# Fourth layer of a hybrid decoder trunk: another instruction order in the S5 layers, and weights asked for at other places

## The chip, the core and the metric

The kernel runs on one core of one Trainium2 chip. The metric is the time of one launch in microseconds (us) on the device; lower is better. The core has a matrix engine (PE; PEld is its weight loading), a vector engine (DVE), a scalar engine (ACT), a general engine (POOL) and a queue engine (SP), from whose queue nearly all DMA transfers of this kernel are issued. Each engine works through its own instructions in the order in which the program holds them, and waits at an instruction whose inputs or buffers are not ready.

## The reference

Four layers act on 512 tokens of width 1024. Layers 0 and 3 are S5 layers (a diagonal complex state space model), layer 1 is HGRN2, layer 2 is attention over a window with sinks. Every layer does `h = h + RMSNorm(branch(RMSNorm(h)))`. The S5 branch, cut to what matters:

```python
proj = h @ w_in                       # 1024 -> 2048
u, z = proj[..., :1024], proj[..., 1024:]
# 64 groups of 16 channels, 64 complex states each; (ar, ai) is the discretised pole
xr, xi = einsum(u, bbr), einsum(u, bbi)
sr, si = associative_scan(complex multiply-add with (ar, ai), (xr, xi), over the tokens)
y = einsum(c_re, sr) - einsum(c_im, si) + d_skip * u
y = gelu(y)
y = y * sigmoid(y @ w_glu + b_glu)
return (y * silu(z)) @ w_out
```

## The kernel before

**Products.** Weights are loaded as float32 (`wraw`). Except in the in-projection of layer 0, which multiplies float32 directly, each weight piece is split in two (`w_conv`, lines 174 to 186): ACT writes a rounded part `whi` (line 182), DVE the rest `wlo` (line 183); the activations are split likewise (`xh`, `xl`), and each product is three matmuls (`whi xh`, `whi xl`, `wlo xh`; `ws_steps`, line 228). A weight chunk is 1024 x 256 in two pieces. The pool holds three `wraw` pieces, four `whi` and four `wlo`: two converted chunks. So a new piece can only be loaded when an older piece has been converted (or, in layer 0, used), and a new chunk can only be converted when the chunk two before it has been used.

**An S5 layer.** The in-projection has 8 chunks: 0 to 3 give `u` in eight blocks of 128 channels (b = 0 to 7), 4 to 7 give the gate `z`. The first four blocks are done in two halves of 256 tokens, because the last 256 tokens are normalised and transposed (`xtp`, then ACT `xh` and DVE `xl`, lines 292 to 298) while PE is already at the first 256. Meanwhile each block of `u` goes through the state space model, in these steps:
- `s5_u`: ACT copies the block out (`ut`), a DMA stores it (`ub`) and another loads it in another layout (`u`).
- `s5_v`: a DMA loads the block's parameters (`prm`), DVE and POOL make coefficients (`q`, `q12b`), DVE makes `vt` in three instructions (lines 727 to 731).
- `s5_taps`: PE `kps` and `ktp`, two `tps` transposes that ACT copies to `v`, DVE `ksb` (line 768), and eight small DMAs that write `ksb` into `toep` (line 773).
- `s5_core`: PE `xps`, DVE `xa` and a scan (`r`, line 835), DVE `spre` (line 845), PE `yps` from `toep`, `u`, `w` and `spre` (lines 858, 860), ACT `ysb`, PE `ytp`, ACT `y`.

After the in-projection comes the gate product with `w_glu` (`s5_glu_first` for its first four output blocks, on `yh`, `yl`), then the out-projection.

**What sets the order.** In the S5 layers the order on PE, DVE, ACT and SP is written by a planner, `Flow`: each step above is a generator that names an engine, an assumed duration and the steps it needs; the planner takes the step that could start first by its own clock and emits its instructions. `Flow.free` holds when each engine is free. The transfers of weights are not steps of their own: `w_load` is emitted wherever `w_next` or `w_conv` is called, and so gets a place in SP's queue by the side. In layer 0 the gate's first weights are asked for by `w_next`, when chunk 6 of the in-projection is taken. In layer 3 `s5_convs` (line 620) plans the conversions of chunks 1 to 7; chunk 0 is converted in the out-projection of layer 2 (line 376). That out-projection is ordered by the general scheduler.

Of the kernel before, what the change touches and what calls it, by code (L numbers as in the profile page):

```python
# [50 lines left out]
class Mark:  # L51


    def __init__(self):
        self.t = None


class Flow:
# [6 lines left out]

    LAG = {"P": 0.4, "V": 0.4, "A": 0.4, "G": 0.4, "D": 4.5}

    def __init__(self):
        self.free = dict.fromkeys(self.LAG, 0.0)
        self.lines = []  # L70

    def add(self, line, rank, t=0.0):
# [36 lines left out]
class Trunk:  # L109
# [86 lines left out]
    def w_next(self, name=None):  # L196
        i = self.wi
        if name is not None:
            assert self.wseq[i][0] == name, (self.wseq[i], name)
        self.wi += 1  # L200
        self.w_conv(i)
        self.w_load(i + 1)
        if self.wseq[i][0].endswith("out") and self.wseq[i][2] == 1:
            return self.wcv.pop(i)
        if not self.plain(i) or self.plain(i + 1):
            self.w_conv(i + 1)
            self.w_load(i + 2)
        return self.wcv.pop(i)

    def w_take(self):  # L210
# [117 lines left out]
    def out_proj(self, L, nxt, h):  # L328
# [8 lines left out]
        def evac(ps, c, tb):  # L337
            junk = self.small.tile([P, 512], mybir.dt.bfloat16, tag="junk", name="junk", bufs=1)
            nc.scalar.activation(out=junk, in_=ps, func=AF.Square, accum_out=ss[tb][:, c:c + 1])  # L339
            f = slice(c * 512, (c + 1) * 512)  # L340
            nc.vector.tensor_tensor(out=yg[:, tb, f], in0=ps, in1=gp[:, f], op=ALU.mult)  # L341
# [18 lines left out]
        with self.wx_pool(L):  # L360
            w = []
            for tbs, cs in (((0, 1), (0, 1)), ((2, 3), (0,))):
                for c in cs:
                    if tbs[0] == 0:
                        w.append(self.w_next())
                    for tb in tbs:
                        ps = self.pj("ops")
                        self.as_(ps, self.g, tb, w[c])
                        evac(ps, c, tb)
                if tbs[0] == 0:  # L370
                    for tb in tbs:
                        finish(tb)
                    if nxt is not None:
                        self.norm_stats(nxt, (0, 1), h)
                    spill(0)
            self.w_conv(self.wi)
            self.w_load(self.wi + 1)
            xt = iter(()) if nxt is None else self.norm_xt(nxt, (0, 1))
            next(xt, None)
            for tb in (2, 3):  # L380
                ps = self.pj("ops")
                for k, _ in enumerate(self.as_steps(ps, self.g, tb, w[1])):
                    if k % 4 == 3:
                        next(xt, None)
                evac(ps, 1, tb)
                finish(tb)
                if nxt is not None:
                    self.norm_stats(nxt, (tb,), h)
# [230 lines left out]

    def s5_convs(self, i0, m):  # L620

        for c in range(1, 8):
            yield "A", 2.1, (m["cd", c - 2],) if c > 1 else ()
            yield "V", 2.6, ()
            self.w_conv(i0 + c)
            self.w_load(i0 + c + 1)
            yield m["cv", c]
# [360 lines left out]
    def layer_s5(self, L):  # L988
        nc, a = self.nc, self.a
        j = L // 3  # L990
# [4 lines left out]
        with self.scratch("left"), self.tc.manual_schedule(engines={E.PE, E.DVE, E.Activation, E.SP}):  # L995
            if L:
                self.s5_open(j)
            m = defaultdict(Mark)
            ps, yh, yl, glu = {}, [], [], []

            flow = Flow()
            i0 = self.wi
            if j == 0:
                flow.add(self.s5_tables(j, m), 0, 5.0)
            else:
                m["ap"].t = 4.5
                flow.add(self.s5_convs(i0, m), 60)
            for b in range(8):
                flow.add(self.s5_core(b, m), 10 * b + 1)
# [632 lines left out]
```

## Time and profile before

| | |
|---|---|
| median of 3 runs | 1119.49 us (1118.13 to 1121.62) |
| the profiled execution's own time | 1116.3 us |
| its span, first to last instruction | 1114.5 us |
| PE busy | 1031.2 us |
| DVE busy | 750.5 us |
| ACT busy | 504.2 us |
| mean granted TensorE clock | 0.973 of full |

The busy share of PE counts an engine that works at half clock as busy, so two things lose time there: stretches in which PE waits, and stretches in which the granted clock is low. Both are read from stretches of the trace, below. The profiled execution took 1.8 us outside its span, and is 3.2 us shorter than the median.

### The profile page before, as it was taken

The page shows a single profiled execution, that of the slowest core. Times are in us where ns is not written, and L with a number is a line of the kernel's source. Part 1 is how long each engine was busy: PE and PEld are TensorE (multiplying, and loading weights), DVE is VectorE, ACT ScalarE, POOL GpSimd, SP SyncE. Part 2 cuts the span into 40 slices and gives each one's busy share as a digit, 9 for nine tenths or more (in the row PEclk, how much of TensorE's full clock was granted, in tenths as well). Part 3 has the DMA queues.
Part 4 walks back from the last instruction along what each step waited for, and adds up shares of the span by engine and source line. Part 5 has one row for each costly group of instructions (what it writes and reads, how often), then busy time and mean ns, then how long its engine had stood idle before and what let it go on. Part 6 is the DMA issues. An engine that isn't in the chain of part 4 may idle for free.

```text
span 1114.5 us, 17031 instructions
## 1 busy us (share of the span) xinstructions
PE 1031.2 (93%) x6480; PEld 822.3 (74%) x6480; DVE 750.5 (67%) x1458; ACT 504.2 (45%) x933; POOL 103.2 (9%) x162
## 2 busy tenths in 40 slices
PE   5999975999999999999999898999997879988997
PEld 4755544778899798998978885666676767766876
DVE  6786759585698777887856565556664468863752
ACT  4344425554452314333244534688743355645540
POOL 2000000030200000000011022100002010100200
PEclk9999988999999999999999999999999889998999
DMA  6574233533432324414153452211125357544331
GB/s 230 137 190 126 74 85 98 171 114 126 143 103 81 114 71 132 144 65 151 61 189 124 122 145 62 74 57 53 61 95 167 117 155 238 173 124 146 104 103 57
DMA packets 70577, 133.31 MB, mean 120 GB/s; under 512 B 28896, under 2 KB 40032, under 8 KB 69472
## 3 DMA queue, kind: packets, MB, share of 16 engines
q1 hardware_dynamic: 65664, 119.04, 34.6%
q10 hardware_dynamic: 4832, 13.19, 3.6%
q8 instruction: 51, 0.84, 0.3%
q14 instruction: 30, 0.25, 0.1%
HBM read 100.51 MB, written 20.15 MB: 108 GB/s over the span
## 4 chain that ended last, share of the span: by engine, by line
PE 63%; DVE 15%; ACT 6%; DMA 6%; issue 5%; SPq 2%; POOL 1%; ACTq 1%; DVEq 0%; POOLq 0%
PE pj L228 26%; PE ops L243 13%; PE zps L243 4%; PE vps L243 3%; PE sps L1120 2%; PE scps L1328 2%; DVE wlo L183 2%; SPq L773 2%; ACT whi L182 2%; PE aops L1364 2%; DMA rsw<-rraw 1%; DMA prm<-in_s_bc 1%; PE ptp L1359 1%; DVE sg L1049 1%; PE yps L858 1%
## 5 line engine op out<-in xcount | busy, mean ns | idle before, releaser
L183 DVE TENSOR_TENSOR wlo<-wraw,whi 128x1024 fp32r<-128x1024 f32 x116 | 143.2, 1251 | 65.0 <-ACT whi L182 56.1
L228 PE MATMUL pj<-xh,whi 128*128 128x512 f32 (+1 forms) x496 | 182.3, 370 | 0.0
L228 PE MATMUL pj<-xl,whi 128*128 128x512 f32 (+1 forms) x496 | 177.9, 360 | 2.5 <-DVE xl L298 2.4
L228 PE MATMUL pj<-xh,wlo 128*128 128x512 f32 (+1 forms) x496 | 177.4, 359 | 0.0
L182 ACT ACTIVATE whi<-wraw 128x1024 fp32r<-128x1024 f32 x116 | 120.7, 1056 | 79.4 <-PE pj L228 38.2
L228 PE MATMUL pj<-xf,wraw 128*128 128x512 f32 (+1 forms) x320 | 116.0, 512 | 0.0
L228 PEld LDWEIGHTS pj<-xh,whi 128*128 128x128 f32 x496 | 96.3, 195 | 16.8 <-issue 5.8
L228 PEld LDWEIGHTS pj<-xl,whi 128*128 128x128 f32 x496 | 96.9, 196 | 14.6 <-DVE xl L298 3.2
L228 PEld LDWEIGHTS pj<-xh,wlo 128*128 128x128 f32 x496 | 96.5, 195 | 13.6 <-issue 1.7
L243 PE MATMUL ops<-whi,gh 128*128 128x512 f32 x256 | 101.6, 398 | 2.7 <-ACT gh L1051 2.2
L243 PE MATMUL ops<-wlo,gh 128*128 128x512 f32 x256 | 100.7, 394 | 1.1 <-DVE wlo L183 1.0
L243 PE MATMUL ops<-whi,gl 128*128 128x512 f32 x256 | 100.5, 395 | 0.0
L228 PEld LDWEIGHTS pj<-xf,wraw 128*128 128x128 f32 x320 | 59.2, 192 | 40.4 <-issue 36.7
L243 PEld LDWEIGHTS ops<-whi,gh 128*128 128x128 f32 x256 | 48.2, 188 | 13.8 <-ACT gh L1051 3.0
L243 PEld LDWEIGHTS ops<-wlo,gh 128*128 128x128 f32 x256 | 48.2, 188 | 13.2 <-DVE wlo L183 2.7
L243 PEld LDWEIGHTS ops<-whi,gl 128*128 128x128 f32 x256 | 48.1, 188 | 11.3 <-DVE gl L1052 0.9
L228 PE MATMUL pj<-yl,whi 128*128 128x512 f32 x128 | 51.0, 399 | 3.5 <-DVE yl L950 3.5
L228 PE MATMUL pj<-yh,whi 128*128 128x512 f32 x128 | 51.3, 401 | 0.5 <-ACT yh L946 0.5
L228 PE MATMUL pj<-yh,wlo 128*128 128x512 f32 x128 | 50.8, 397 | 0.0
L341 DVE TENSOR_TENSOR yg<-ops,gpost 128x512 f32<-128x512 f32 x32 | 21.9, 688 | 36.9 <-ACT junk L339 36.6
L243 PE MATMUL vps<-wlo,xh 128*128 128x256 f32 x160 | 45.3, 283 | 0.0
L243 PE MATMUL vps<-whi,xl 128*128 128x256 f32 x160 | 45.3, 283 | 0.0
(279 smaller groups left out, 2106.4 us busy)
## 6 DMA issues: line engine op xcount, KB each, us to landing
wraw<-in_s_in SPq DMA_DIRECT2D x32, 512.0 KB, 6.3
wraw<-in_hg_in SPq DMA_DIRECT2D x32, 512.0 KB, 3.6
wraw<-in_at_in SPq DMA_DIRECT2D x20, 512.0 KB, 4.2
wraw<-in_s_glu SPq DMA_DIRECT2D x16, 512.0 KB, 3.8
wraw<-in_s_out SPq DMA_DIRECT2D x16, 512.0 KB, 3.5
hd<-h SPq DMA_DIRECT2D x6, 1024.0 KB, 4.0
prm<-in_s_bc SPq DMA_DIRECT2D x16, 256.0 KB, 4.6
ub<-ut SPq DMA_DIRECT2D x16, 256.0 KB, 4.2
```

Of the source, the lines that this page charges most:

```text
L182: nc.scalar.activation(out=hi, in_=raw, func=AF.Copy)
L183: nc.vector.tensor_tensor(out=lo, in0=raw, in1=hi.bitcast(F32), op=ALU.subtract)
L228: self.nc.tensor.matmul(ps, lhsT=l[k // 4][:, k % 4, c], rhs=r[:, k, n0:n1], start=k == 0 and n == 0, stop=k == KB - 1 and n == len(terms) ...
L243: self.nc.tensor.matmul(ps, lhsT=l[:, k, c], rhs=r[k // per][:, k % per, :], start=k == 0 and n == 0, stop=k == KB - 1 and n == 2)
L341: nc.vector.tensor_tensor(out=yg[:, tb, f], in0=ps, in1=gp[:, f], op=ALU.mult)
L773: nc.sync.dma_start(out=toep[128 - n:128, jj, :, :], in_=ksb[0:n].rearrange("p a g h -> p (a g) h"))
L858: nc.tensor.matmul(o, lhsT=u[:, g, :], rhs=d["toep"][:, :, g, :], start=True, stop=False)
L1049: nc.vector.tensor_tensor(out=sg, in0=sg, in1=y[:, k, :], op=ALU.mult)
L1120: nc.tensor.matmul(ps[:, c, :], lhsT=k[:, c * 128:c * 128 + 128], rhs=q4[:, c, :, 1, :], start=True, stop=True)
L1328: nc.tensor.matmul(ps[:, bb, lo:256], lhsT=self.q[r, 4 * p + 2 * b2 + bb, qs], rhs=self.k[r, p, ks], start=True, stop=True)
L1359: nc.tensor.transpose(tp[:, f, bb, :], sm[:, bb, f * 128:f * 128 + 128], self.ident)
L1364: nc.tensor.matmul(ops[64 * i:64 * i + 64].rearrange("p b q -> p (b q)"), lhsT=self.v[:, n - 1 + f, kv * 64:kv * 64 + 64], rhs=pts[i][:, f ...
```

## The change

Four edits.
1. In layer 0, `w_next` no longer asks for a chunk that is not of the in-projection when it takes chunk 6; the gate's first chunk is then asked for when chunk 7 is taken.
2. In the out-projection ahead of layer 3, the second chunk of the in-projection (chunk 1) is converted and the third (chunk 2) asked for; `s5_convs` then starts at chunk 2.
3. In layer 3 the planner starts with ACT busy until 12.0 and DVE until 13.0 of its clock.
4. The tables of layer 3 (`m["ap"]`) count as there from 12.0 on, instead of 4.5.

```diff
-    def __init__(self):
+    def __init__(self, **busy):
         self.free = dict.fromkeys(self.LAG, 0.0)
+        self.free.update(busy)
...
-        if not self.plain(i) or self.plain(i + 1):
+        if not self.plain(i):
             self.w_conv(i + 1)
             self.w_load(i + 2)
+        elif self.plain(i + 1):
+            self.w_conv(i + 1)
+            if self.plain(i + 2):
+                self.w_load(i + 2)
         return self.wcv.pop(i)
...
             self.w_conv(self.wi)
             self.w_load(self.wi + 1)
+            if nxt == 3:
+                self.w_conv(self.wi + 1)
+                self.w_load(self.wi + 2)
...
-        for c in range(1, 8):
+        m["cv", 1].t = 0.0
+        for c in range(2, 8):
             yield "A", 2.1, (m["cd", c - 2],) if c > 1 else ()
...
-            flow = Flow()
+
+            flow = Flow() if j == 0 else Flow(A=12.0, V=13.0)
...
-                m["ap"].t = 4.5
+                m["ap"].t = 12.0
```

In layer 0 only SP's queue changes, at one place. Before, the two pieces of the gate's first chunk (`s_glu`) stand ahead of `u` and of the eight `toep` transfers of block 4:

```order
L692 DMA rotf<-rot 64x1024
L152 DMA wraw<-in_s_glu 128x1024 x2
L806 DMA u<-ub 128x512
L773 DMA toep<-ksb 16x128
L773 DMA toep<-ksb 32x128
L773 DMA toep<-ksb 48x128
L773 DMA toep<-ksb 64x128
L773 DMA toep<-ksb 80x128
L773 DMA toep<-ksb 96x128
L773 DMA toep<-ksb 112x128
L773 DMA toep<-ksb 128x128
L706 DMA prm<-in_s_bc 128x512
```

Now, at the same place of the queue:

```order
L701 DMA rotf<-rot 64x1024
L815 DMA u<-ub 128x512
L782 DMA toep<-ksb 16x128
L782 DMA toep<-ksb 32x128
L782 DMA toep<-ksb 48x128
L782 DMA toep<-ksb 64x128
L782 DMA toep<-ksb 80x128
L782 DMA toep<-ksb 96x128
L782 DMA toep<-ksb 112x128
L782 DMA toep<-ksb 128x128
L715 DMA prm<-in_s_bc 128x512
L153 DMA wraw<-in_s_glu 128x1024 x2
```

The weight request moved behind ten transfers, and everything behind it keeps its place. PE, DVE and ACT have the same order as before in layers 0, 1 and 2.

In layer 3 the order of all engines changes. On DVE at its entry stood, behind the last instruction of layer 2 (`xs`), the coefficients and `vt` of block 0 among the sixteen `xl` of the last 256 tokens:

```order
L277 TENSOR_SCALAR xs<-h,rs_r 128x1024
L713 TENSOR_TENSOR q_7805<-prm,co 128x256
L715 TENSOR_TENSOR q_7805<-q_7805,q12b 128x256
L727 TENSOR_TENSOR vt<-ap,q_7805 128x1024
L298 SCALAR_TENSOR_TENSOR xl<-xtp,gpre,xh 128x128 x8
L730 TENSOR_TENSOR t_7874<-ap,q_7805 128x1024
L731 TENSOR_TENSOR vt<-vt,t_7874 128x1024
L298 SCALAR_TENSOR_TENSOR xl<-xtp,gpre,xh 128x128 x8
L713 TENSOR_TENSOR q_7981<-prm,co 128x256
```

Now:

```order
L282 TENSOR_SCALAR xs<-h,rs_r 128x1024
L303 SCALAR_TENSOR_TENSOR xl<-xtp,gpre,xh 128x128 x16
L722 TENSOR_TENSOR q_7926<-prm,co 128x256
L724 TENSOR_TENSOR q_7926<-q_7926,q12b 128x256
L736 TENSOR_TENSOR vt<-ap,q_7926 128x1024
L739 TENSOR_TENSOR t_7973<-ap,q_7926 128x1024
L740 TENSOR_TENSOR vt<-vt,t_7973 128x1024
L184 TENSOR_TENSOR wlo<-wraw,whi 128x1024 x2
L722 TENSOR_TENSOR q_8068<-prm,co 128x256
```

All sixteen `xl` come first. On ACT the sixteen `xh` come first likewise. On PE, block 0's `kps` and first `tps` moved from the first half block behind the `xl` to the last one. ACT's and DVE's conversions of chunks 0 and 1 stand at the same places as before: the scheduler already had chunk 1's in the out-projection; what is new there is that SP asks for chunk 2.

SP's queue around block 0's `toep` in layer 3, before (the row behind the last one shown is the second of the eight `toep` transfers):

```order
L613 DMA rotf<-sd 64x1024 x4
L152 DMA wraw<-in_s_in 128x1024 x2
L617 DMA w<-sd 128x1024
L706 DMA prm<-in_s_bc 128x512
L802 DMA ub<-ut 128x8x64
L617 DMA w<-sd 128x1024
L773 DMA toep<-ksb 16x128
```

and now:

```order
L621 DMA rotf<-sd 64x1024 x4
L811 DMA ub<-ut 128x8x64
L625 DMA w<-sd 128x1024
L153 DMA wraw<-in_s_in 128x1024 x2
L715 DMA prm<-in_s_bc 128x512
L815 DMA u<-ub 128x512
L811 DMA ub<-ut 128x8x64
L815 DMA u<-ub 128x512
L153 DMA wraw<-in_s_in 128x1024 x2
L625 DMA w<-sd 128x1024
L811 DMA ub<-ut 128x8x64
L782 DMA toep<-ksb 16x128
```

Block 1's `prm` moved behind a weight request (chunk 3), and block 0's `toep` behind a further one (chunk 4) and the transfers of `u` for blocks 0 and 1. Block 2's `prm` stands behind that `toep` in both; before, one weight request lies between them, now none.

## Rows read from the trace of the kernel before

**Rows 1.** The page's busy times by engine, and of its costliest groups the two of the weight conversion: line, engine, operation, shapes, count, busy us, mean ns of one, idle time before it and what ended most of that.
```profile
PE 1031.2 (93%) x6480; PEld 822.3 (74%) x6480; DVE 750.5 (67%) x1458; ACT 504.2 (45%) x933; POOL 103.2 (9%) x162
...
L183 DVE TENSOR_TENSOR wlo<-wraw,whi 128x1024 fp32r<-128x1024 f32 x116 | 143.2, 1251 | 65.0 <-ACT whi L182 56.1
...
L182 ACT ACTIVATE whi<-wraw 128x1024 fp32r<-128x1024 f32 x116 | 120.7, 1056 | 79.4 <-PE pj L228 38.2
```

**Rows 2.** PE in time around block 4's `yps` in layer 0: start us, length us, engine, line, operation, out<-in, shapes, count, and in brackets the idle time just before with what ended it.
```profile
140.85 1.12 PE L228 MATMUL pj<-xf,wraw 128*128 128x512 f32 x2
149.59 0.69 PE L858 MATMUL yps<-toep,u 128*64 128x128 f32 x4 [7.62 <-DMA toep<-ksb]
```

**Rows 3.** SP's queue in time in the same stretch: start us, time that the issue took with its wait, line, transfer, count.
```profile
122.83 19.52 SPq L152 DMA_DIRECT2D wraw<-in_s_glu  x2
142.40 0.42 SPq L806 DMA_DIRECT2D u<-ub  x1
142.91 5.00 SPq L773 DMA_DIRECT2D toep<-ksb  x8
```

**Rows 4.** The chain of waits in the same stretch: start us, length us, what.
```profile
147.32 1.88 DMA toep<-ksb
149.19 12.11 issue
...
175.51 2.01 ACT whi L182 x2
```

**Rows 5.** DVE in time in the same stretch, columns as in rows 2.
```profile
131.84 0.29 DVE L768 TENSOR_TENSOR ksb<-ktp,dmx 128x128 f32<-128x128 f32 x1 [6.01 <-PE ktp L762]
...
141.37 0.68 DVE L845 TENSOR_TENSOR spre<-r,rsw 128x504 f32<-128x504 f32 x1
...
148.51 0.68 DVE L684 TENSOR_TENSOR rot<-rot,rt 128x512 f32<-128x512 f32 x1
...
161.31 0.29 DVE L768 TENSOR_TENSOR ksb<-ktp,dmx 128x128 f32<-128x128 f32 x1 [12.11 <-issue]
```

**Rows 6.** Stretches: from:to, length, then busy us (x instructions) of PE, PEld, DVE, ACT, POOL, then the granted clock as a share of full, DMA share and GB/s.
```profile
149.50:154.00 4.50, 4.41 (x36) 4.11 (x37) 0.00 (x0) 0.60 (x1) 0.00 (x0) 0.51 0.17 51
...
862.00:874.00 12.00, 8.65 (x47) 7.17 (x48) 7.91 (x17) 4.09 (x12) 0.62 (x1) 0.50 0.23 89
...
905.40:911.00 5.60, 5.51 (x29) 3.83 (x31) 4.95 (x7) 0.74 (x2) 0.00 (x0) 0.50 0.57 138
...
1015.40:1021.00 5.60, 5.52 (x13) 4.38 (x14) 4.24 (x8) 2.09 (x5) 0.00 (x0) 0.51 0.44 157
```

**Rows 7.** PE in time at the entry of layer 3, columns as in rows 2; the first row is the last matmul of the first half blocks.
```profile
856.68 0.28 PE L228 MATMUL pj<-xh,wlo 128*128 128x256 f32 x1
861.83 1.11 PE L292 MATMUL xtp<-cst,xs 128*128 128x128 f32 x4 [4.87 <-DVE xl L298]
864.44 1.12 PE L292 MATMUL xtp<-cst,xs 128*128 128x128 f32 x4 [1.50 <-DVE xl L298]
...
867.54 0.58 PE L228 MATMUL pj<-xl,whi 128*128 128x256 f32 x1 [1.76 <-DVE xl L298]
```

**Rows 8.** DVE in time at the same place, columns as in rows 2.
```profile
852.28 0.89 DVE L277 TENSOR_SCALAR xs<-h,rs_r 128x1024 f32<-128x1024 f32 x1 [2.12 <-POOL rs_r L254]
856.53 0.43 DVE L713 TENSOR_TENSOR q<-prm,co 128x256 f32<-128x256 f32 x1 [3.37 <-DMA prm<-in_s_bc]
```

**Rows 9.** Stretches, columns as in rows 6: from the end of the first half blocks to the end of the second half blocks (96 matmuls of 256 columns) in layers 1, 2 and 3.
```profile
303.96:320.85 16.89, 14.31 (x106) 14.03 (x107) 14.73 (x59) 12.60 (x25) 0.00 (x0) 0.90 0.17 55
620.04:637.78 17.74, 14.35 (x107) 14.11 (x107) 8.33 (x21) 9.95 (x22) 0.00 (x0) 0.90 0.21 55
856.96:884.90 27.94, 19.73 (x148) 17.92 (x149) 16.68 (x28) 10.43 (x25) 2.40 (x3) 0.76 0.43 123
```

**Rows 10.** PE in time at the end of the last of these stretches (`kps` and `tps` at full clock), then at the next long wait; columns as in rows 2.
```profile
883.71 0.64 PE L745 MATMUL kps<-vt,c 128*32 128x128 f32 x16
...
884.74 0.60 PE L754 MATMUL tps<-cst,vt 128*128 128x128 f32 x4
...
905.49 1.08 PE L745 MATMUL kps<-vt,c 128*32 128x128 f32 x16 [5.32 <-DVE vt L731]
```

**Rows 11.** SP's queue between these, columns as in rows 3.
```profile
885.35 1.24 SPq L152 DMA_DIRECT2D wraw<-in_s_in  x2
886.69 0.39 SPq L706 DMA_DIRECT2D prm<-in_s_bc  x1
```

**Rows 12.** DVE's wait for that transfer, columns as in rows 2.
```profile
894.61 0.42 DVE L713 TENSOR_TENSOR q<-prm,co 128x256 f32<-128x256 f32 x1 [10.79 <-DMA prm<-in_s_bc]
```

**Rows 13.** DMA issues of layer 3 up to 1010 us: transfer, queue, count, KB each, median us from issue to landing.
```profile
prm<-in_s_bc SPq DMA_DIRECT2D x8, 256.0 KB, 6.3
```

**Rows 14.** What SP's queue waited for from 840 to 1010 us: us in total, times, longest us.
```profile
SPq L773 <- DVE ksb L768: 22.7, 7, 6.0
...
SPq L152 <- DVE wlo L183: 11.3, 3, 6.4
```

**Rows 15.** The rest of layer 3's in-projection: a stretch (columns as in rows 6).
```profile
915.00:1011.00 96.00, 88.62 (x810) 70.20 (x808) 66.87 (x84) 58.27 (x92) 8.61 (x11) 1.00 0.61 185
```

**Rows 16.** PE in time where the gate product begins, columns as in rows 2.
```profile
1011.53 0.49 PE L228 MATMUL pj<-yh,whi 128*128 128x512 f32 x1 [0.49 <-ACT yh L946]
1015.48 0.80 PE L228 MATMUL pj<-yl,whi 128*128 128x512 f32 x1 [3.45 <-DVE yl L950]
```

## The prediction, made before the changed kernel was run

> **What bounds the kernel now.** I read the page first, then the waits in stretches, then the engines in time around each long wait. The page says PE is busy 93% of the span [rows 1], so a change of order can only win where PE waits or works at a low clock. I listed PE's waits over the two S5 layers, since only these change. In layer 0 there are two long ones. The first, 7.62 us, ends when block 4's `toep` lands [rows 2]; the second is DVE's own work, and no edit touches it. In layer 3 there are four places: the entry, where 4.87, 1.50 and 1.76 us end with an `xl` [rows 7]; a 5.32 us wait for `vt` [rows 10]; 7.4 us of small waits from 915 to 1011 (96 less 88.62) [rows 15]; and 0.49 and 3.45 us where the gate product begins [rows 16]. After each long one the granted clock is about half, 1.2 in place of 2.4 GHz, for some microseconds of work [rows 6].
>
> **Layer 0: the request moves behind `toep`.** The reader should see in SP's rows that the request for the gate weights stood in the queue from 122.83 for 19.52 us, until 142.4 [rows 3]. That is just behind the last matmul of chunk 6, which ends at 141.97 [rows 2]: the second piece needs that chunk's buffer. Behind it waited `u` and `toep`, although `ksb`, the source of `toep`, was done at 132.1 [rows 5]. So `toep` was issued from 142.91 for 5.00 us, landed 1.88 us after the last issue [rows 3, 4], and PE stood still from 141.97 to 149.59.
>
> Now `toep` comes first. It can be issued from 132.1 to 137.1 and lands near 139.0, 3 us before PE comes to `yps`. `spre`, which `yps` also needs, ends at 142.05 [rows 5], so `yps` starts at 142.0 to 142.1. That removes 7.5 us. The half clock behind the wait goes too, since PE no longer stops: 4.41 us of work at 0.51 [rows 6] is 2.2 us. Sum: 9.7 us.
>
> Does it carry to the end? Chain and DVE rows agree: DVE stands idle for 12.11 us until the next `ksb`, at 161.31, which hangs on PE [rows 4, 5]; from there DVE is the engine that everything waits for. All of that starts earlier by what PE wins. The next thing late would be DVE itself, whose work before ends at 149.2; with 9.7 us won `ksb` comes at 151.6, so 2.4 us are left and the cap of the gain is 12.1. The request itself now waits behind `prm`, but for the same buffer until the same 141.97, and its data are first used by a conversion at 175.51 [rows 4], 166 with the gain, so I cost it at nothing; without that cover it would cost its landing, a few us. Behind the waiting request stand block 7's `u` and block 6's rotations; both wait for things that are done at 142 or later anyhow. If `toep`'s landing took longer by its slack of 3 us, the gain would shrink from there; I bound it from below at 6 us.
>
> **Layer 3, the entry.** Before, DVE ends `xs` at 853.17 and could make the first `xl`, but it holds `q` first, which waits until 856.53 for `prm`, and then `vt` [rows 8]. PE is through its first half blocks at 856.96 and waits [rows 7]. Layers 1 and 2 begin in the same way with nothing between the `xl`: there the second half blocks end 16.89 and 17.74 us after the first ones; in layer 3 it is 27.94 us [rows 9]. I take 17.3 for the new order, with its own dip of the clock in it (0.90 in both). Layer 3's 27.94 held block 0's `kps`, two `tps`, `ktp` and block 1's `kps`; now `kps` and one `tps` stay in it, 1.0 us, and about 1.2 us of the others come later (0.64 and 0.60 each at full clock [rows 10]; overlaps make it a little less). Gain: 27.9 - 17.3 - 1.0 - 1.2 = 8.4 us, by the two examples 8.0 to 8.8; the half blocks end near 875.3.
>
> **Layer 3, the next wait.** Before, block 2's `prm` is issued at 886.69, behind two pieces of weights [rows 11], DVE waits for it until 894.61 [rows 12], and PE until 905.49. Cost: 5.32 us and 5.51 us of work at half clock [rows 6], 2.8 us; 8.1 together. Now block 2's `prm` stands behind block 0's `toep`, this behind `ksb`, and that behind the conversion of chunk 3, which can begin when chunk 1's last product is done at 875.3. ACT first copies a `v`, which I put at 878.0, two matmul groups and a copy later; two `whi` of 1.06 to 880.1; the last `wlo`, 1.25 [rows 1], to 881.4; the first `vt` instruction, of the same size, to 882.6; `ksb` 0.3 to 882.9; eight issues 5.0 to 887.9; `u`, then `prm` from 888.5. With the median of 6.3 us [rows 13] it lands at 894.8. DVE's `q` stands ahead of `spre` of block 0, some 3.3 us in all (0.42 twice with POOL between, three of 0.68): `spre` at 898.1. PE did 48 wide matmuls and what lay between them from 884.90 to 900.17, 0.32 us each; now 63 come before that `yps`, so PE is there at 895.4 and waits 2.7 us. With the 7.9 us that the same transfer took here [rows 11, 12] it is 4.3, with 4 us nothing. Next, block 1's `toep` stands behind the request for chunk 5, which waits for the conversion of chunk 4: a wait that can reach the 6.4 us of the longest such wait in this layer [rows 14]; I take 3. With one half-clock dip of 2.8 the new waits are 8.5 in place of 8.1: I take no change, from 8 us better (both hidden) to 6 worse (both at their ends, two dips).
>
> On the clock: here it fell to half after the waits of 4.87, 5.32 and 3.45 us [rows 6, 7, 10, 16]. The Trainium skill, TensorE: Matmul & The Clock Gate, section "What's actually happening", says that the throttled state is the default and activity releases it; by that rule a new wait can bring the dip back even where it is shorter than the old one, and both waits would be paid with a dip, 2.8 us more than in my sum.
>
> **Layer 3, the rest.** The same work in another order over some 96 us, and 3.9 us with 5.52 at half clock (2.7) at the end. DVE is 70% busy and PE 92% [rows 15], so neither side is tight. I take no change, 5 us either way. The earlier request for chunk 2 is worth nothing by itself: it adds two issues to a queue that stands until the layer's tables may be written.
>
> **Sum.** -9.7 - 8.4 = -18.1 us on the profiled execution's 1116.3 gives 1098.2. That execution is 3.2 us below the median of the runs, so I forecast 1101 for the median. Its own range, with 6 to 12.1 in layer 0, 8.0 to 8.8 at the entry and the two open terms within 5 us together, is 1094 to 1109.
>
> **Rivals.**
> - *Only layer 0 counts.* The entry's gain is handed back in layer 3, because the waits for `prm` and `toep` hang on SP and DVE and not on PE. For it: 22.7 us of SP's waits there are for `ksb` and 11.3 for conversions [rows 14]. Against it: these waits also start from PE's progress, which is earlier. Time: 1119.5 - 9.7 = 1110.
> - *The new order works throughout.* The two new waits are hidden (8 us) and half of the small ones go (4 us): 1101 - 12 = 1089. For it: no work of the state space model stands ahead of an `xl` any more. Against it: the planner still gives the weights no time in SP's queue, and those are what the two waits hang on.
> - *Slower: weight requests block `toep` in layer 3.* The mechanism of layer 0 returns there, since in SP's new order a request stands within five rows ahead of `toep` in most blocks (the part on the change shows the first). Each such block costs what it cost in layer 0, 9.7 us. Two are 19.4 and eat the gain; from three on, 1101 + 29 = 1130, the kernel is slower. For it: SP asks for `toep` only behind them (the part on the change). Against it: of the old order's waits for conversions the longest was 6.4 us. The Trainium skill, Trace Analysis, section "What "DMA-bound" means", names the issuing engine's sequencer as a bound of its own when its track is solid; eight issues of 5.0 us for `toep` [rows 3] are 40 us in a layer of 170, so the trace does not show it solid.
> - *The change does not free `toep`.* Something else in front of it in SP's queue holds it until 142. Against it: once the request was out, `u` and `toep` were issued without a further wait, and `ksb` had been done for ten us [rows 3, 5]. Layer 0 then gives nothing: 1119.5 - 8.4 = 1111.
>
> **How the numbers follow.** Forecast 0.46, only layer 0 0.22, works throughout 0.20, slower 0.07, does not free 0.05. A measurement here can tell 0.3%, about 3.4 us, from no change. The first three and the last lie below 1116 with nearly all their weight; I leave 0.03 of "only layer 0" for a loss in layer 3 that cancels: faster 0.90, same 0.03, slower 0.07. The range reaches from the second rival to a little beyond the first: 1089 to 1112.
>
> **What would show it.** Layer 0: PE's wait of 7.62 us gone, `toep` issued near 132, the next `ksb` near 152 instead of 161, the clock full there. Layer 3: DVE's sixteen `xl` without `vt` between, about 17 us from half blocks to half blocks; a wait of 2 to 4 us at the first `yps`, released by `spre`, with DVE waiting for `prm` before. Wrong would be a wait for `toep` in layer 0 that stays, or PE waits in layer 3 that add up to more than before's 25 us.

## The result, and the profile after

The changed kernel takes 1093.64 us (median of 4 runs, 1091.99 to 1095.69); the kernel before took 1119.28 beside it (4 runs, 1118.13 to 1121.62). The ratio is 0.9769, with a 95% interval of 0.9746 to 0.9792: 25.6 us faster. The profiled execution took 1091.99 us, its span is 1090.2 us (before: 1114.5), the mean granted clock 0.982 (before: 0.973). The forecast was 1101 with a range of 1089 to 1112.

The page's busy times, to hold against [rows 1]:

```profile
PE 1025.8 (94%) x6480; PEld 817.1 (75%) x6480; DVE 750.4 (69%) x1458; ACT 505.2 (46%) x933; POOL 101.5 (9%) x162
```

PE executes the same 6480 matmuls and is busy 5.4 us less, which fits less work at half clock; the other 18.9 us of the span were PE standing idle. So the question is which waits went.

**Layer 0.** SP's queue in time (start us, time that the issue took with its wait, line, transfer, count), against [rows 3]:

```profile
132.01 5.00 SPq L782 DMA_DIRECT2D toep<-ksb  x8
137.12 0.52 SPq L715 DMA_DIRECT2D prm<-in_s_bc  x1
137.69 4.50 SPq L153 DMA_DIRECT2D wraw<-in_s_glu  x2
```

`toep` is issued at 132.01 instead of 142.91, and the request for the gate weights, now behind it, still ends only at 142.19: it waits for the same buffer as before. PE in time at that place, against [rows 2]:

```profile
140.71 1.13 PE L233 MATMUL pj<-xf,wraw 128*128 128x512 f32 x2
141.76 0.44 PE L867 MATMUL yps<-toep,u 128*64 128x128 f32 x4
```

No bracket stands behind `yps`: the wait of 7.62 us is gone. DVE, against the last of [rows 5]:

```profile
151.45 0.29 DVE L777 TENSOR_TENSOR ksb<-ktp,dmx 128x128 f32<-128x128 f32 x1 [2.40 <-issue]
```

The next `ksb` comes at 151.45 instead of 161.31, and of DVE's idle 12.11 us before it 2.40 are left.

**Layer 3.** Stretches of the changed kernel (columns as in rows 6): the first is the one behind layer 0's old wait, the second runs from the end of the first half blocks to the end of the second [rows 9], the others follow the three long waits that are left in layer 3.

```profile
149.50:154.00 4.50, 4.50 (x42) 2.62 (x42) 2.44 (x5) 2.18 (x4) 1.16 (x2) 1.00 0.62 126
...
844.36:862.20 17.84, 15.87 (x124) 13.76 (x125) 10.40 (x19) 8.77 (x19) 0.19 (x1) 1.00 0.57 161
...
898.00:901.50 3.50, 3.43 (x33) 3.29 (x33) 3.46 (x4) 0.00 (x0) 0.00 (x0) 0.55 0.86 213
...
953.50:957.00 3.50, 3.41 (x22) 2.48 (x22) 3.33 (x6) 0.39 (x1) 0.62 (x1) 0.50 0.36 118
...
988.00:992.00 4.00, 3.40 (x29) 3.07 (x30) 4.00 (x7) 1.30 (x4) 0.00 (x0) 0.50 0.35 125
```

The granted clock is the column behind POOL's: full in the first two stretches, which stood at 0.51 and 0.76 before, and about half in the other three. PE in time (the first row at the entry, against [rows 7]; then the new order's long waits, against [rows 10, 16]):

```profile
846.88 0.66 PE L297 MATMUL xtp<-cst,xs 128*128 128x128 f32 x4 [1.96 <-DVE xl L303]
...
882.36 0.44 PE L869 MATMUL yps<-w,spre 128*64 128x128 f32 x4 [0.28 <-DVE spre L854]
...
898.07 0.69 PE L867 MATMUL yps<-toep,u 128*64 128x128 f32 x4 [2.69 <-DMA toep<-ksb]
...
953.59 1.08 PE L754 MATMUL kps<-vt,c 128*32 128x128 f32 x16 [3.66 <-DVE vt L740]
...
988.60 0.70 PE L869 MATMUL yps<-w,spre 128*64 128x128 f32 x4 [5.28 <-DVE spre L854]
```

The entry's waits of 4.87, 1.50 and 1.76 us have become one of 1.96. Block 0's `yps` waits 0.28 us, block 1's 2.69. The two long waits further on are new; in return the gate product's first matmuls no longer wait 3.45 us for `yl`. All of PE's listed waits behind the last `xs` ahead of layer 3 add up to 16.5 us, where before they were 26.8.

### The profile page after: what moved, and what is told of

Same layout as the page of the kernel before. It is cut to its first block, busy times and chain, and to the rows that moved or that the text cites. A ratio compares the mean times of both kernels' runs of the same rounds, so it can differ in the third digit from the quotient of the medians.

```text
span 1090.2 us, 17036 instructions
## 1 busy us (share of the span) xinstructions
PE 1025.8 (94%) x6480; PEld 817.1 (75%) x6480; DVE 750.4 (69%) x1458; ACT 505.2 (46%) x933; POOL 101.5 (9%) x162
## 4 chain that ended last, share of the span: by engine, by line
PE 66%; DVE 16%; ACT 6%; DMA 5%; issue 4%; POOL 1%; SPq 1%; ACTq 1%; DVEq 0%; POOLq 0%
PE pj L233 27%; PE ops L248 13%; PE zps L248 4%; DVE wlo L184 3%; PE sps L1130 3%; PE scps L1338 2%; PE vps L248 2%; ACT whi L183 2%; PE aops L1374 2%; PE yps L867 2%; PE yps L869 2%; PE ptp L1369 1%; DMA rsw<-rraw 1%; DVE sg L1059 1%; PE tps L763 1%
## 5 line engine op out<-in xcount | busy, mean ns | idle before, releaser
L233 PE MATMUL pj<-xl,whi 128*128 128x512 f32 (+1 forms) x496 | 175.4, 355 | 0.8 <-DVE xl L303 0.6
L233 PE MATMUL pj<-xh,wlo 128*128 128x512 f32 (+1 forms) x496 | 175.2, 354 | 0.0
L233 PEld LDWEIGHTS pj<-xl,whi 128*128 128x128 f32 x496 | 94.7, 191 | 13.2 <-DVE xl L303 2.2
```

Of the source, the lines that this page charges most:

```text
L233: self.nc.tensor.matmul(ps, lhsT=l[k // 4][:, k % 4, c], rhs=r[:, k, n0:n1], start=k == 0 and n == 0, stop=k == KB - 1 and n == len(terms) ...
```

## How the time splits over the kernel

DVE's rows in time give two landmarks that every kernel here has: the first `xs` of layer 1, and the last `xs` ahead of layer 3 (852.28 before [rows 8]). They cut a span into three legs: layer 0, layers 1 and 2, layer 3. In the changed kernel they are these:

```profile
265.27 1.42 DVE L282 TENSOR_SCALAR xs<-h,rs_r 128x1024 f32<-128x1024 f32 x2 [2.28 <-POOL rs_r L259]
...
839.68 0.88 DVE L282 TENSOR_SCALAR xs<-h,rs_r 128x1024 f32<-128x1024 f32 x1 [2.12 <-POOL rs_r L259]
```

The table has all fourteen traces; the experiments are described below.

| kernel | median us | ratio to before | layer 0 | layers 1, 2 | layer 3 |
|---|---|---|---|---|---|
| before | 1119.2 to 1120.4 | 1 | 274.0 | 578.3 | 262.2 |
| changed | 1093.64 | 0.9769 | 265.3 | 574.4 | 250.5 |
| changed, run again | 1095.99 | 0.9798 | 265.4 | 582.5 | 249.5 |
| edit 1 alone | 1110.54 | 0.9911 | 263.9 | 581.5 | 263.0 |
| half of the request moved | 1112.22 | 0.9925 | 264.8 | 579.9 | 262.1 |
| edits 2 to 4 | 1105.86 | 0.9864 | 273.9 | 579.5 | 249.3 |
| edit 2 alone | 1119.97 | 1.0004 | 273.1 | 579.0 | 265.6 |
| edits 3 and 4 | 1124.77 | 1.0047 | 274.6 | 579.3 | 271.5 |
| edits 2 and 4 | 1115.03 | 0.9968 | 273.4 | 580.9 | 261.3 |
| edits 2 and 4, requests planned | 1098.15 | 0.9821 | 273.8 | 583.0 | 243.4 |
| changed, states first | 1094.47 | 0.9790 | 264.9 | 577.1 | 248.9 |
| changed, requests planned | 1090.64 | 0.9751 | 265.0 | 579.0 | 246.2 |
| changed, both trials | 1088.57 | 0.9729 | 265.5 | 576.6 | 243.1 |
| changed without edit 3, requests planned | 1089.54 | 0.9731 | 265.1 | 579.6 | 243.3 |

Leg 1 has two values and nothing between: 273.1 to 274.6 without edit 1 (mean 273.8), 263.9 to 265.5 with it (mean 265.0). That is 8.8 us. Leg 3 is 262.1 to 263.0 where layer 3 is as before (mean 262.5) and 249.3 to 250.5 where it is as changed (mean 249.8): 12.7 us. Leg 2 holds the same 3496 matmuls in every kernel but that with edits 3 and 4, which does 18 of them later, and lies anywhere from 574.4 to 583.0.

## The experiments

**Edit 1 alone.**

```diff
-        if not self.plain(i) or self.plain(i + 1):
+        if not self.plain(i):
             self.w_conv(i + 1)
             self.w_load(i + 2)
+        elif self.plain(i + 1):
+            self.w_conv(i + 1)
+            if self.plain(i + 2):
+                self.w_load(i + 2)
```

> The kernel before with only the later request for the gate weights (layer 0's edit); layer 3 stays as before. Theory: the request stood in SP's queue ahead of toep because its second piece waited for a buffer; behind toep it costs nothing, so PE's wait of 7.62 us goes with the half clock behind it. The trace of the changed kernel puts DVE's work after it 9.85 us earlier; alone the edit then gives 9.0 to 10.5 us, a time of about 1109.5, and layer 3's entry still lasts 27.9 us from the first half blocks to the second. Rival A: the further 2.7 us that appeared in layer 2 belong to this edit: 12 to 13 us, 1107, with the shift growing from 9.85 to 12.5 between 660 and 690 us in this trace too. Rival B: part of layer 0's gain is lost again at layer 3's entry, because DMA landings there do not move with PE: 5 to 8 us.

Measured: 1110.54 us, ratio 0.9911 (0.9886 to 0.9936), 9.7 us below the 1120.27 of the kernel before beside it. Layer 0's leg has its gain, layer 3's (263.0) none, and the stretch from half blocks to half blocks still has waits of 4.92 and 1.51 us for `xl`. Rival A falls: layers 1 and 2 took 581.5 us here, not less than before. Layer 3's leg shows nothing lost, so rival B falls too.

**Half of the request moved.** The first piece of the gate's chunk, whose buffer is free, stays ahead of `toep`; only the second, which needs chunk 6's, moves.

```diff
+    late = False
...
-        for v in range(pieces):
+        for v in range(len(have), pieces):
+            if (name, j, c, v) == ("s5_glu", 0, 0, 1) and not self.late:
+                self.late = True
+                return
```

> The kernel before with the request for the first gate chunk left where it was, but cut in two: the first piece, whose buffer is free, is asked for at the old place, and only the second, whose buffer is chunk 6's, behind block 5's toep. Theory (the wait for the buffer blocks the queue, not the request as such): toep is issued near 134.5 (one more issue of 2.3 us ahead of it than in the changed kernel) and lands near 141.5 before PE comes; gain 9 to 10.5 us, as in the run with the whole request moved. Rival (the issues and the bytes themselves delay toep, wherever the buffer stands): the gain is about half, 4 to 6 us, with a wait for toep of 3 us or more left at 142.

Measured: 1112.22 us, ratio 0.9925 (0.9897 to 0.9952), and layer 0's leg is 264.8 us, like with the whole request moved: 8.1 us by the medians and 9.0 by the mean of the legs, at the lower end of the 9 to 10.5 expected. SP's queue of this kernel:

```profile
122.32 0.56 SPq L157 DMA_DIRECT2D wraw<-in_s_glu  x1
123.41 0.79 SPq L811 DMA_DIRECT2D u<-ub  x1
131.64 5.01 SPq L778 DMA_DIRECT2D toep<-ksb  x8
136.76 0.52 SPq L711 DMA_DIRECT2D prm<-in_s_bc  x1
141.50 0.33 SPq L157 DMA_DIRECT2D wraw<-in_s_glu  x1
```

The first piece costs the queue 0.56 us and delays nothing; the second sits until 141.5, when its buffer comes free. Of the 19.52 us of [rows 3], all but about one was that one buffer. (That one issue takes 2.3 us, as the expectation had it, was wrong: the 4.50 us of the changed kernel are mostly this wait too.)

**Edits 2 to 4, without edit 1.**

```diff
-            flow = Flow()
+            flow = Flow() if j == 0 else Flow(A=12.0, V=13.0)
...
-                m["ap"].t = 4.5
+                m["ap"].t = 12.0
```

with edit 2 as in the change.

> The kernel before with all edits but the request's: chunk 1 converted and chunk 2 asked for in the out-projection, tables at 12.0, ACT and DVE busy at entry. Theory: the gains add, layer 3 gives what the changed kernel's trace has beyond layer 0 and layer 2, 11 to 13 us, a time of about 1107.5; PE still waits 7.6 us for toep in layer 0, the sixteen xl are uninterrupted, the stretch from half blocks to half blocks lasts 17.8 us. If layer 2's 2.7 us belong to these edits: 14 to 15 us. Rival (layer 3's gain needs layer 0's, because parameters and rotations land relative to another clock): under 8 us.

Measured: 1105.86 us, ratio 0.9864 (0.9817 to 0.9912), 14.4 us between the medians. Layer 3's leg is 249.3 us, layer 0's is as before. The two ratios multiply to 0.9911 x 0.9864 = 0.9776; the changed kernel has 0.9769. The terms add, and the two layers don't need each other. The 14.4 us is at the upper end of what was expected, with an interval that reaches from 10 to 20 us; the leg says 12.9.

**Edit 2 alone.**

```diff
+            if nxt == 3:
+                self.w_conv(self.wi + 1)
+                self.w_load(self.wi + 2)
...
-        for c in range(1, 8):
+        m["cv", 1].t = 0.0
+        for c in range(2, 8):
```

> The kernel before with only the edit that converts chunk 1 and asks for chunk 2 in the out-projection of layer 2; the planner's numbers stay as before. Theory: DVE and PE keep the order of before at the entry, q and a vt stand between xs and the xl, PE waits there as before, and nothing is won: ratio to before 0.997 to 1.003, the stretch from half blocks to half blocks near 28 us. Rival (layer 3's gain comes from the earlier request of chunk 2, so that its conversion and the queue behind it come sooner): 5 us or more faster, though q still stands ahead of the xl.

Measured: 1119.97 us, ratio 1.0004 (0.9980 to 1.0028). By itself the earlier request is worth nothing. (In its one trace layer 3's leg is even 3.1 us longer than the mean of the three with layer 3 as before; the medians don't show that loss.)

**Edits 3 and 4 without edit 2.** The planner's numbers only; chunk 1 is then converted behind the busy time.

> The kernel before with only the planner's numbers (ACT busy to 12, DVE to 13, tables from 12.0), without converting chunk 1 in the out-projection. Its conversion is then planned behind the busy time and stands, with block 0's q and whole vt, ahead of the first of the sixteen xl. Theory: what counts at the entry is that nothing stands between xs and the xl; here q still waits for prm until about 856.5, two wlo of 1.25 and three vt instructions of 1.2 follow, the first xl comes near 863 instead of 861.8 with two wlo's time between, and the second halves end 2 to 5 us later than before: a loss at the entry, the whole between 1117 and 1124 (0 to 5 us slower). Rival (the busy times alone make the better order, the conversion's place does not matter): 8 us or more faster than before.

Measured: 1124.77 us, ratio 1.0047 (1.0022 to 1.0071): slower, as expected, but the expectation had the wrong wait. It spoke of a late first `xl`; the long wait is PE's, earlier, for chunk 1 itself. PE and then ACT in time:

```profile
859.43 0.58 PE L229 MATMUL pj<-xh,whi 128*128 128x256 f32 x1 [7.50 <-ACT whi L183]
```

```profile
858.03 0.40 ACT L719 ACTIVATE c<-prm,cst 128x128 f32<-128x128 f32 x1 [4.58 <-DMA prm<-in_s_bc]
858.34 1.99 ACT L183 ACTIVATE whi<-wraw 128x1024 fp32r<-128x1024 f32 x2
```

The conversion stands behind a coefficient that waits for `prm`, and PE runs out of converted weights in the middle of the first half blocks. So edit 2, worth nothing alone, is what allows edit 3.

**Edits 2 and 4, without the busy times.** As the changed layer 3, but with `Flow()`.

> The kernel before with chunk 1's conversion in the out-projection and the tables' time at 12.0, but without ACT and DVE taken as busy at entry. By the order of the program DVE's sixteen xl then stand together too; what differs from the layer 3 edits together is the planner's order from block 2 on. Theory (the gain is the uninterrupted xl at the entry): 9 to 15 us faster than before, like the layer 3 edits together (14.4 us by the medians), with a stretch of about 17.8 us. Rival (it is the busy times that place requests and toep well after the entry): at least 6 us less than those, with a wait of 3 us or more for prm or toep between 880 and 910 that the changed kernel doesn't have.

Measured: 1115.03 us, ratio 0.9968 (0.9947 to 0.9988), 4.2 us faster by the medians: about 10 less than with edit 3 (12.0 less by layer 3's legs, 261.3 and 249.3). My theory falls here, and the rival stands, though the wait that it named, 3 us or more between 880 and 910, was 2.46 us there and the longer ones came later. The entry is as good as in the changed kernel (the sixteen `xl` start at 856.10, 1.8 us behind the last `xs`, with nothing between), and the gain is given back later. The waits of PE from 850 to 1040 us in this kernel (us in total, times, longest):

```profile
PE yps L862 <- DMA toep<-ksb: 15.5, 5, 3.9
PE kps L749 <- ACT z L940: 3.8, 1, 3.8
PE xtp L292 <- DVE xl L298: 2.0, 1, 2.0
```

Five waits for `toep`. SP's queue ahead of one of them, DVE's `ksb` there, and PE:

```profile
920.88 6.21 SPq L152 DMA_DIRECT2D wraw<-in_s_in  x2
927.14 5.01 SPq L777 DMA_DIRECT2D toep<-ksb  x8
```

```profile
922.14 0.27 DVE L772 TENSOR_TENSOR ksb<-ktp,dmx 128x128 f32<-128x128 f32 x1
925.50 2.36 DVE L183 TENSOR_TENSOR wlo<-wraw,whi 128x1024 fp32r<-128x1024 f32 x2 [3.09 <-ACT whi L182]
```

```profile
934.50 0.44 PE L862 MATMUL yps<-toep,u 128*64 128x128 f32 x4 [3.81 <-DMA toep<-ksb]
```

`ksb` is done at 922.4, but SP holds the request until `wlo` frees a raw buffer, and issues `toep` 4.7 us later; PE then waits 3.81. This is layer 0's mechanism, the one that the prediction carried as its slower rival. Three of the five waits (3.81, 3.46 and 3.92 us) have such a request directly ahead of `toep`; ahead of the first stands a `u` that was issued only at 890.46, and the last, of 1.86 us, follows a late `ksb`.

**The same with requests planned.** Each request becomes a step of its own behind its conversion, so the planner knows that it holds the queue.

```diff
             self.w_conv(i0 + c)
+            yield m["cv", c]
+            yield "D", 0.4, ()
             self.w_load(i0 + c + 1)
-            yield m["cv", c]
```

> The kernel that kept only 3.6 us of layer 3's gain (chunk edit and tables' time, ACT and DVE free at entry), with each request for a weight chunk made a step of its own behind its conversion. In that kernel PE waited for toep five times, 2.46, 3.81, 3.46, 3.92 and 1.86 us. Theory (there the requests, which wait in SP's queue for conversions, stood ahead of toep; the busy times at entry gain because they make the planner put toep first): with requests planned, toep stands ahead of them and the waits for toep fall to 3 us or less in all; time 1103 to 1108, like the layer 3 edits together (ratio 0.984 to 0.992). Rival (without the busy times DVE itself is late with ksb, vt and spre, and toep is late with them): the waits stay at 8 us or more, 1111 to 1116.

Measured: 1098.15 us, ratio 0.9821 (0.9794 to 0.9847), faster than either forecast. PE's waits in the same stretch as above:

```profile
PE pj L228 <- DVE yl L955: 3.3, 1, 3.3
PE xps L826 <- ACT v L761: 3.1, 2, 2.8
PE xtp L292 <- DVE xl L298: 2.0, 1, 2.0
```

No wait for `toep` is left of 15.5 us, and layer 3's leg falls from 261.3 to 243.4 us. The rival (DVE late by itself) falls. Other steps moved with the requests, so not all of the 17.9 us is shown to be the five waits and their half clock.

**Two trials at the changed kernel's waits, and both.** "States first" puts the gate product's second conversion behind block 7's states; "requests planned" is the edit above, on the changed kernel.

```diff
-            yield "V", 2.6, (m["rest"],)
+            yield "V", 2.6, (m["rest"],) + ((m["states", 7],) if early else ())
```

> The changed kernel with the gate product's second conversion and its steps put behind block 7's states, so that spre of block 7 isn't made late by two whi and two wlo ahead of it (PE waited 5.28 us there). Theory (what stands ahead of rsw and spre on ACT and DVE is all of that wait): rsw comes about 2 us earlier, wlo of 2.5 us goes behind spre, PE's wait falls to 1 to 3 us; the conversion late by as much may cost the gate product up to 2 us: 0 to 4 us faster than the changed kernel, 1090 to 1094. Rival (the wait only moves to the gate product, as before the change, where yl was late): the same time, with a new wait of 3 us or more at its first matmuls.

> The changed kernel with each request for a chunk of the in-projection made a step of its own for the planner, on the DMA queue, so that SP's order puts toep of block 1 ahead of the request for chunk 5 (PE waited 2.69 us for that toep at 898). Theory (the request blocked it, as in layer 0): that wait goes with its half clock, 3 to 5 us; the planner moves other steps of layer 3 too, 4 us either way: 1085 to 1096. Rival (toep is late because ksb is): the wait stays at 2 us or more.

> The changed kernel with both trials together: requests planned as their own step, and the gate product's second conversion behind block 7's states. Theory (the two waits, 2.69 us for toep and 5.28 us for spre, have causes of their own): no wait for toep at block 1 as with the first alone, the wait for spre near 3.2 us as with the second alone; 2 to 5 us faster than the changed kernel in the same call. Rival (what is won ahead is waited for at the gate product): within 1 us of the first trial alone, 1090.6.

Measured, in ratios to before: 0.9790 (0.9753 to 0.9826), 0.9751 (0.9717 to 0.9785), 0.9729 (0.9702 to 0.9756). The first alone can't be told from the changed kernel. Its wait for `spre` fell from 5.28 to 3.19 us (1 to 3 were expected), and no new wait of 3 us, as its rival had it, stands behind that one:

```profile
989.44 0.69 PE L869 MATMUL yps<-w,spre 128*64 128x128 f32 x4 [3.19 <-DVE spre L854]
```

The second removed the wait of 2.69 us for block 1's `toep`, as expected: SP asked for it at 888.68, right behind its `ksb` (done at 888.65), where in the changed kernel 2.0 us lay between the two (889.21 and 891.25). With both, the kernel took 1088.57 us beside 1095.99 for the changed kernel, 7.4 us faster where 2 to 5 were expected, with 3.04 us of the wait for `spre` left. That is more than the two alone seem to give (by the legs 0.9 and 3.6 us alone, 6.7 together), but the first one's interval holds 4 us either way.

**The changed kernel again.**

> The changed kernel again, unchanged, beside the two runs below on the same chip. Theory and rivals alike: 1091 to 1097 us, ratio to before 0.974 to 0.980. It tells in a second trace which numbers belong to the program (layer 0's shift of 9.85 us, the stretch of 17.8 us, the waits for toep, vt and spre in layer 3) and which to one execution (layer 2's 2.7 us, prm's landing of 3.1 us).

Measured: ratio 0.9798 (0.9771 to 0.9826). Layer 0's and layer 3's legs come back within 1.0 us, layers 1 and 2 take 582.5 us instead of 574.4. The waits of layer 3 come back as well: 1.96, 2.67, 3.66 and 5.00 us. `prm` of block 2 is issued at 884.49 and used at 887.61, 3.1 us, as in the first trace.

**Requests planned, without the busy times.** The run with edits 2 and 4 and planned requests, plus edit 1; the only difference between the two kernels lies in SP's queue in layer 0.

> The changed kernel with requests planned as their own step, and with ACT and DVE no longer taken as busy at entry; it differs from the run with the tables' time and planned requests only by layer 0's edit. Theory (the terms add; with requests planned the busy times have nothing left to do): the 9.9 us of layer 0 come off that run's ratio of 0.9821, so 0.9733, near 1089 us, like the run with both trials. Rival (the busy times are still worth something, or the terms don't add): 1094 us or more.

Measured: 1089.54 us, ratio 0.9731 (0.9705 to 0.9756). The terms add once more, and with the requests planned the busy times of edit 3 have nothing left to do. The fair neighbour is the changed kernel with requests planned, which differs in the busy times alone: its ratio is 0.9751, the same within the intervals, and layer 3's leg is 246.2 us with them and 243.3 without, so in these two traces they rather cost something.

## Why the prediction was right, and where its sizes were off

**Layer 0 (forecast 9.7 us).** Right in every step: `toep` issued at 132.01 (forecast 132.1), `yps` at 141.76 (142.0), no dip (clock 1.00), the next `ksb` at 151.45 (151.6), 2.40 us left on DVE (2.4). At that `ksb` the trace is 9.86 us ahead; at layer 1's first `xs` 8.7, and over all traces 8.8. The half request shows the cause: not the request as such, but the buffer for which it waits at the head of the queue. About a microsecond is lost on the way, where nothing was forecast to hold it. The traces show where. In both kernels PE waits 9.11 us for a `vt`, still 9.85 us apart; then comes half clock, and the clock's mean over the next 8 us is 0.80 before and 0.62 after the change (PE before and after, then the two stretches, columns as in rows 6):

```profile
188.21 1.08 PE L745 MATMUL kps<-vt,c 128*32 128x128 f32 x16 [9.11 <-DVE vt L731]
178.36 1.08 PE L754 MATMUL kps<-vt,c 128*32 128x128 f32 x16 [9.11 <-DVE vt L740]
...
188.21:196.21 8.00, 7.92 (x96) 6.45 (x97) 7.66 (x10) 4.35 (x7) 0.00 (x0) 0.80 0.01 3
178.36:186.36 8.00, 7.93 (x91) 6.51 (x91) 6.44 (x8) 3.08 (x6) 0.00 (x0) 0.62 0.01 2
```

So the half clock lasted about 3.2 us before and 6.0 now, and the shift falls from 9.85 to 8.66 us by the next `yps` that waits. All eight traces with edit 1 have the longer dip, and so have two of the six without it; why it is longer is open. The two rivals "does not free `toep`" and "only layer 0" fall with the runs of edit 1 alone and of edits 2 to 4.

**The entry of layer 3 (forecast 8.4).** The stretch is 17.84 us instead of 27.94, with `kps` and one `tps` in it as forecast; the forecast was 18.3. So 0.5 us more came: 8.9. The bound taken from layers 1 and 2 was good, though they don't begin quite as the prediction says: in layer 1 small instructions of DVE do stand between the `xl`, and in both layers PE waited longer at this place than it now does in layer 3 (PE in the trace before, layers 1 and 2):

```profile
306.54 1.26 PE L292 MATMUL xtp<-cst,xs 128*128 128x128 f32 x8 [2.59 <-DVE xl L298]
...
623.41 1.09 PE L292 MATMUL xtp<-cst,xs 128*128 128x128 f32 x8 [3.37 <-DVE xl L298]
```

Behind these waits the clock fell (0.64 from 308 to 312 us, 0.62 from 624 to 628); behind the 1.96 us in layer 3 it did not, and so the dip that the bound held did not come. The Trainium skill, TensorE: Matmul & The Clock Gate, section "What's actually happening", has the throttled state as the default, from which the prediction drew that a shorter wait can bring the dip back too. The traces agree in part: after the wait of 1.96 us the clock stayed at 1.00, after 2.69 us its mean was 0.55.

**The next wait (forecast 0.4 worse) is the term that was mis-sized.** The prediction read the steps up to the issue of `prm` to within a microsecond each, and the issue itself exactly. Its clock is 12.60 us behind the changed trace's (852.28 less 839.68, the last `xs`); with that, `prm` goes out at 875.90 + 12.60 = 888.5, the forecast. But it took the landing at 6.3 us, the median of [rows 13], and 3.1 us came, twice (SP, then DVE):

```profile
875.90 0.38 SPq L715 DMA_DIRECT2D prm<-in_s_bc  x1
...
879.01 0.42 DVE L722 TENSOR_TENSOR q<-prm,co 128x256 f32<-128x256 f32 x1 [3.78 <-DMA prm<-in_s_bc]
...
881.62 0.68 DVE L854 TENSOR_TENSOR spre<-r,rsw 128x504 f32<-128x504 f32 x1
```

So `spre` was ready 3.2 us before its forecast, `yps` waited 0.28 us instead of 2.7, and no dip came there. The landing in [rows 11, 12] took 7.9 us with weight pieces issued on both sides of it; the new place has none beside it. Block 1's `prm` in the changed kernel, issued right behind two pieces, took 5.2 us:

```profile
858.13 0.42 SPq L715 DMA_DIRECT2D prm<-in_s_bc  x1
...
863.30 0.42 DVE L722 TENSOR_TENSOR q<-prm,co 128x256 f32<-128x256 f32 x1 [4.44 <-DMA prm<-in_s_bc]
```

The eight `prm` of the changed kernel landed 2.9 to 8.0 us after their issue, and in its second trace each came back within 0.8 us. So the landing belonged to the place in the queue, and a median over eight places was a poor guess for one of them. That weight pieces ahead lengthen it is argued from the queue and was not tried; pieces behind it do not by themselves, since one `prm` of the kernel before, at 955.85, landed in 3.0 us with two right behind it. Block 1's `yps` waited 2.69 us for `toep` behind the request for chunk 5, where 3 were forecast, with about 3.1 us of work at half clock behind it, some 1.5 us lost. Together the new waits cost 0.28 + 2.69 + 1.5 = 4.5 us, not 8.5: 3.6 better than the old order's 8.1.

**The rest of layer 3 (forecast 0).** By difference: the leg's 12.7 us less 8.9 and 3.6 is 0.2. Behind that zero are large terms that cancel: 3.66 us for `vt` and 5.28 us for `spre`, with some 5.6 and 4.7 us at half clock behind them, about 14 us in all, against 14.0 us in the small waits of [rows 15] (7.4) and at the gate product of [rows 16] (3.9, and 2.7 for its half clock). That they cancel is luck: the prediction took no change, and named neither of the two new waits. The 5.28 us have two causes that the prediction did not name: on ACT two `yh` and two `whi` stand ahead of `rsw`, on DVE two `wlo` ahead of the rotations. Putting them later took 2.1 us off it; the other 3.2 stayed.

**The sum.** Forecast 18.1 us, with the next wait's 0.4 taken as nothing; the legs of layers 0 and 3 give 8.8 + 12.7 = 21.5. Of the 3.4 us between them 3.6 are the next wait, 0.5 the entry and 0.2 the rest, less 0.9 in layer 0. The medians say 25.6 and, beside the second run, 23.9. In the profiled pair 3.9 us came from layers 1 and 2, which the second trace shows to be that execution's luck. Where the last 2 to 4 us of the medians lie is open: only profiled executions have a trace, and single runs of the kernel before went from 1111 to 1125 us. Two things more on the sum. The prediction's terms add up to an upper end of 1110.5 for its own range, not 1109; nothing hangs on that. And the measured time lies between the forecast of 1101 and the rival "the new order works throughout" (1089), which came half true: the first of its two waits was hidden (0.28 us), the second was not (2.69).

**The slower rival** was a real mechanism with too high a price. In the changed kernel it was left with the one wait of 2.69 us. In the order without the busy times three waits of 3.5 to 3.9 us had a request ahead of `toep`, not 9.7 each, and that order gave only 4 of the 14 us that edits 2 to 4 gain by the medians; planning the requests removed all its waits for `toep` and brought the gain back. So where the requests stand decided the size of layer 3, and the prediction gave the credit of edit 3 to the entry alone. The Trainium skill, Perfetto Trace Analysis, section "What "DMA-bound" means", looks for an issuing engine whose track is solid. In the run without the busy times `toep` was late while SP's eight issues took 5.01 us as ever: the queue stood at one request that waited for a buffer, so `toep` was late without the queue being full of issues.

**Not tried.** The wait of 3.66 us for `vt`, which all orders with edits 2 and 3 have, and the waits for `v` and `yl` (3.3 us each) that are left in the last kernel.

## What to carry to other kernels

A transfer that waits for its buffer holds everything behind it in its queue (19.52 us here), so look for requests ahead of urgent small transfers, and ask whether the wait is for the buffer: moving only the piece that waits gave the whole gain. Where a planner sets the order, let it plan each request as a step; that one edit did here what the assumed busy times do, and some 6 us more by layer 3's leg. For an unseen transfer look for the landing of one with the same neighbours in its queue, rather than the median of a layer, which was 6.3 us here where 3.1 came. Price the half clock behind a wait with a spread: it lasted 3.2 to 6.0 us here, and both ends stood behind the same wait of 9.11 us.

## What the runs showed that was not expected

- Layers 1 and 2, with nearly the same instructions in every kernel, took from 574.4 to 583.0 us over fourteen executions, 8.1 us apart for the same program. One piece of it is PE's wait for the rotated `q` in layer 2: 1.4 us in the first trace of the changed kernel, 2.8 before, 3.5 in the second trace. The rest was not located. A gain of a few microseconds is better read from the leg that holds the edit than from the span.
- The issue of one 512 KB weight piece took 0.56 and 0.33 us of SP's queue when its buffer was free, and up to 19.5 us for two when it was not.
